# Pooling operands a block ahead, RWKV own products ahead of the chain

## The chip, the cores and the metric

The kernel runs on one core of one Trainium2 chip. Five engines work side by side: TensorE (PE), VectorE (DVE), ScalarE (ACT), GpSimd (POOL) and SyncE (SP), which issues the DMAs. The metric is the device time of one execution in microseconds, as a median of several runs.

## The reference, cut to what matters

One layer of a streaming encoder on x of 4096 tokens x 1024 features, float32. One projection x @ w_in feeds four mixers of 256 columns each (RWKV-7, pooling, mLSTM, retention); their outputs are gated, concatenated, projected again and normalised. Of the two mixers that the change touches:

```python
def pool_mix(u, w_grp, scale):       # u (B,S,256), windows 2, 4, 8, 16, one per group of 64 columns
    means = [(hi[..., sl] - lo) / min(t1, win) ...]          # trailing means, from a running sum
    d = concatenate(means) - u
    return einsum('bsgc,gcd->bsgd', d, w_grp) * scale

def step(state, inp):                # RWKV-7, one token, per head: state is 64 x 64
    sa = einsum('bhvk,bhk->bhv', state, -kk_t)
    state = state * w_t + sa * ab_t + v_t * k_t
    return state, einsum('bhvk,bhk->bhv', state, r_t)
```

The pooled result is multiplied by z * sigmoid(z) of a gate projection.

## The kernel before, in words

Tokens are cut into 16 blocks of 256 (`TB`). The stages follow one another: pooling (0 to 246.6 us), retention (to about 660), mLSTM (to about 1242), RWKV (to about 1957, with a tail of the embedding work to 2090), embedding and output. Every float32 product of the projections is taken with operands split in two parts, high and low (`hi`, `lo`): ScalarE casts the raw tile to `hi`, VectorE or POOL subtracts it to give `lo` (`fetch`), and three matmuls make one product (`dense`, lines 145 to 147). All DMAs are issued by SP in one order. The order of instructions on each engine is set by a scheduler that follows the program's order and priorities; `soon()` raises a priority, `keep` holds the program's order.

*Pooling.* `dense(b)` loads x of the block (`load_x`, four tiles), makes `zu` (48 matmuls) and twice `zpg` (24 each, with the gates of the mLSTM); `mix(b)` makes the trailing sums `s` on POOL, the differences `dp` on VectorE, `yp` on TensorE (8), multiplies by the gate `spg` on VectorE and by `pl_scale` on POOL, and stores y. Beside this, from block 2 on, one job a block of the list `todo`: the right operands of retention (`rB1`, `rB2`, `rB4` to `rB7`) are quarters of `w_rt` and differences of quarters. `sums` loads four quarter rows, forms four differences on POOL and stores them to DRAM (`T4` to `T7`); `right` reads quarters and differences back and splits them. `sums` also does this for `w_ml`, to be read by the mLSTM.

*RWKV.* Iteration i runs the string `ORDER` from left to right. Words name a stage with the lag of its block (`la`, `k`, `r`, `g`, `v` are dense groups through the `mm` PSUM banks, `n/2` takes two pieces); `vt` turns v and copies it to the tile `SAV`; `s`, `p` make `st`, `gp`; `inv`, `iv`, `pt`, `px`, `pu`, `py` invert a triangular matrix X in steps; `C` is one step of the chain of block i-2. A chain has four chunks of 64 tokens with three steps each: (1) `ry`: the state against `AR`, and the chunk's own products `g1` x `SAV` added (line 258 names all matmuls of RWKV), then the copy `R`; (2) `sa`, copied into `SAV`; (3) `ds`, the new state S, and the second half of `ry` to Y. `g1` of the own products are 64x64 blocks: the chunk's parity `e` chooses the array quadrant.

Of the kernel before, what the change touches and what calls it, by code (L numbers as in the profile page):

```python
# [42 lines left out]
class Trunk:  # L43
# [27 lines left out]
    def fetch(self, hi, lo, src, nm, eng):  # L71
# [4 lines left out]
        if self.spare % 2:  # L76
# [10 lines left out]
    def weights(self, name, g0, w=G, pool=None, bufs=5, gates=False):  # L87
# [30 lines left out]
    def load_x(self, b, more=None, between=None):  # L118

        his, los = [], []  # L120
        for k in range(0, KT, 2):
            p, n = (more, 3) if more is not None and (4 * b + k // 2) % 8 in (1, 4, 7) else (self.xp, XB)
# [69 lines left out]
    def _rwkv_out(self, es):  # L192
# [344 lines left out]
        def pt(b):  # L537
# [3 lines left out]
            V.transpose(out=Z.rearrange("p a c -> p (a c)"), in_=X.rearrange("p a c -> p (a c)"))  # L541
# [7 lines left out]
            A.copy(out=TD[:, :, 0:16], in_=t)  # L549
# [3 lines left out]
        def px(b):  # L553
# [14 lines left out]
        def pu(b):  # L568
# [3 lines left out]
            V.transpose(out=Z.rearrange("p a c -> p (a c)"), in_=X.rearrange("p a c -> p (a c)"))  # L572
# [5 lines left out]
            for e in range(2):  # L578
                A.copy(out=T[low(e)], in_=t[low(e)])
# [4 lines left out]
        def py(b):  # L584
# [5 lines left out]
            for e in range(2):  # L590
                V.tensor_copy(out=X[top(e), :, 32:64], in_=t[top(e)])
            yield 0.6
        def chain(b):

            eC, bon, AR, SAV, ST, g1, sg = (bl[b][n] for n in ("eC", "bon", "AR", "SAV", "ST", "g1", "sg"))
            Y = p2.tile([P, 2, G], F32, name=f"Y{b}", tag="Y")
            for c in range(4):
# [19 lines left out]
                with self.soon():  # L617
# [3 lines left out]
                    A.copy(out=SAV[cc][bs, e], in_=sa[bs].rearrange("p a v -> p (a v)"))  # L621
                yield True
# [92 lines left out]
    def pooling(self, es):  # L715
        nc, tc, a = self.nc, self.tc, self.a
        pool = lambda name, **kw: es.enter_context(tc.tile_pool(name=name, reuse_waits="tile", **kw))
        ws = pool("pws", bufs=1)
# [3 lines left out]
        p2 = pool("p2", bufs=2)  # L722
        self.mm = pool("pmm", bufs=4, space=PSUM)
# [12 lines left out]
        scale = self.load(cp, "pl_scale", a["pl_scale"].partition_broadcast(P))  # L736
        gbias = self.load(cp, "gbias", a["gbias"].partition_broadcast(P))
# [20 lines left out]
        def mix(b):  # L758
# [29 lines left out]
            V.scalar_tensor_tensor(out=Yp, in0=yp, scalar=0.5, in1=spg, op0=ALU.mult, op1=ALU.mult)  # L788
# [932 lines left out]
```

## Time and profile before

| | before |
|---|---|
| median of 3 runs | 2820.2 us (2818.15 to 2822.43) |
| the profiled execution | 2818.06 us, span 2816.3 us |
| TensorE busy | 2683.2 us, 95% |
| VectorE busy | 2166.8 us, 77% |
| ScalarE, POOL busy | 1104.5 us (39%), 1160.2 us (41%) |
| DMA moved | 281.14 MB |

A busy time counts the instructions of an engine in a stretch; matmuls are pipelined, so a start and the next start tell more than a duration. A row `A <- B` of a wait names the engine that stood idle and what released it. The time between the span and the execution, 1.8 us, lies outside the recorded program.

### The profile page before, as it was taken

Reading aid. Unit: us, or ns where it says so; the run is one execution under the profiler, and the core shown is the slowest. Engines: PE = TensorE matmul, PEld = TensorE weight load, DVE = VectorE, ACT = ScalarE, POOL = GpSimd, SP = SyncE. Lnnn points to the kernel's source line nnn. Section 1 sums busy time; section 2 is a strip of 40 time slices with the busy share of each in tenths; the row PEclk is TensorE's granted clock in tenths of the full one; section 3 lists DMA queues with packets and bytes.
Section 4 is the critical chain, followed back from the end, with each engine's and each line's share of the span. In section 5 each row is a group of like instructions: output and inputs, shape, how many; then the busy total and the mean of one; then the engine's idle time right before and its main releaser. Section 6 shows DMA issues by size and latency. Waiting matters only on the chain.

```text
span 2816.3 us, 57672 instructions
## 1 busy us (share of the span) xinstructions
PE 2683.2 (95%) x21940; PEld 2408.3 (86%) x21940; DVE 2166.8 (77%) x5239; ACT 1104.5 (39%) x2644; POOL 1160.2 (41%) x1295
## 2 busy tenths in 40 slices
PE   8899999998999999988999999999998999999997
PEld 7798888887899999978999999999887888778885
DVE  5666888887777787876888888888555566689997
ACT  2423222233666666653344434444222333422221
POOL 6555555553443344421232323333234111256665
PEclk9899999999999999989999999999999999999998
DMA  7753212213311111231111111113347444633431
GB/s 230 225 152 110 64 57 61 68 53 104 107 61 57 53 57 57 81 104 31 49 39 49 39 49 39 50 39 98 118 161 232 146 135 137 224 141 145 162 143 67
DMA packets 250501, 281.14 MB, mean 100 GB/s; under 512 B 69488, under 2 KB 166512, under 8 KB 250224
## 3 DMA queue, kind: packets, MB, share of 16 engines
q1 hardware_dynamic: 250224, 277.46, 31.4%
q8 instruction: 172, 2.82, 0.4%
q14 instruction: 105, 0.86, 0.1%
HBM read 209.69 MB, written 67.70 MB: 98 GB/s over the span
## 4 chain that ended last, share of the span: by engine, by line
PE 65%; DVE 15%; DMA 5%; POOL 4%; issue 4%; ACT 2%; SPq 0%; POOLq 0%; DVEq 0%; ACTq 0%
PE ry L258 3%; PE zqk L145 2%; PE zqk L147 2%; PE zqk L146 2%; DVE ro L1613 2%; DVE ro L1592 1%; PE sa L258 1%; PE zg L154 1%; DVE ro L1595 1%; PE zra L1406 1%; PE zg L156 1%; PE zg L155 1%; POOL ro L1596 1%; PE zrb L1407 1%; PE zrc L1406 1%
## 5 line engine op out<-in xcount | busy, mean ns | idle before, releaser
L1371 ACT CAST Ah<-xr 128x512 fp32r<-128x512 f32 x189 | 117.2, 621 | 278.6 <-PE zrb L1407 58.7
L1372 DVE TENSOR_TENSOR Al<-xr,Ah 128x512 fp32r<-128x512 f32 x135 | 99.0, 734 | 78.6 <-ACT Ah L1371 75.0
L651 POOL TENSOR_TENSOR SAV<-SAV,bon 64x256 f32<-64x256 f32 x64 | 42.7, 668 | 282.9 <-PE ry L258 272.4
L146 PE MATMUL zqk<-xl,wh_w_ml 128*128 128x256 f32 x512 | 148.7, 290 | 0.3 <-DVE xl L1062 0.3
L145 PE MATMUL zqk<-xh,wh_w_ml 128*128 128x256 f32 x512 | 148.2, 290 | 0.8 <-ACT xh L1061 0.8
L147 PE MATMUL zqk<-xh,wl_w_ml 128*128 128x256 f32 x512 | 147.7, 289 | 0.0
L85 DVE TENSOR_TENSOR xl<-rawx,xh 128x512 fp32r<-128x512 f32 x148 | 123.1, 835 | 31.6 <-ACT xh L84 30.7
L84 ACT CAST xh<-rawx 128x512 fp32r<-128x512 f32 x148 | 91.9, 621 | 139.6 <-DMA rawx<-in_xT 71.0
L1372 POOL TENSOR_TENSOR Al<-xr,Ah 128x512 fp32r<-128x512 f32 x54 | 70.9, 1313 | 132.8 <-ACT Ah L1371 72.0
L1596 POOL TENSOR_TENSOR ro<-ro,ln_b 128x512 f32<-128x512 f32 x64 | 100.7, 1594 | 53.8 <-DVE ro L1595 53.8
L849 POOL TENSOR_TENSOR rot<-rot,sw 128x256 f32<-128x256 f32 x64 | 69.4, 1084 | 93.9 <-DVE sw L848 89.1
L146 PEld LDWEIGHTS zqk<-xl,wh_w_ml 128*128 128x128 f32 x512 | 98.1, 192 | 2.3 <-DVE xl L1062 0.5
L145 PEld LDWEIGHTS zqk<-xh,wh_w_ml 128*128 128x128 f32 x512 | 97.9, 191 | 2.5 <-ACT xh L1061 1.0
L147 PEld LDWEIGHTS zqk<-xh,wl_w_ml 128*128 128x128 f32 x512 | 98.0, 191 | 1.1
L433 DVE SCALAR_TENSOR_TENSOR g<-gp,rc,c_rmask 128x128 f32<-128x128 f32 x256 | 70.9, 344 | 31.5 <-PE gp L258 31.5
L145 PE MATMUL zu<-xh,wh_w_pl 128*128 128x256 f32 x256 | 78.9, 308 | 15.7 <-ACT xh L84 10.0
L1391 POOL TENSOR_TENSOR xr<-xr,xr 128x512 f32<-128x512 f32 x27 | 35.2, 1302 | 141.2 <-DVE xr L1388 141.1
L146 PE MATMUL zu<-xl,wh_w_pl 128*128 128x256 f32 x256 | 78.1, 305 | 11.0 <-DVE xl L85 11.0
L1171 DVE SCALAR_TENSOR_TENSOR xc<-zc,c_convw,xc 128x256 f32<-128x256 f32 x192 | 87.6, 505 | 0.5
L634 DVE SCALAR_TENSOR_TENSOR S<-ds,eC,Se 64x64 f32<-64x64 f32 x256 | 72.4, 283 | 19.1 <-PE ds L258 14.4
L258 PE MATMUL ry<-SAV,g 64*64 64x64 f32 (+1 forms) x1024 | 83.5, 223 | 0.0
L659 POOL TENSOR_TENSOR Y<-Y,SAV 64x256 f32<-64x256 f32 x64 | 50.2, 784 | 75.7 <-DVE Y L655 65.8
(1127 smaller groups left out, 10578.9 us busy)
## 6 DMA issues: line engine op xcount, KB each, us to landing
rawx<-in_xT SPq DMA_DIRECT2D x148, 256.0 KB, 3.3
xr<-in_xT SPq DMA_DIRECT2D x108, 256.0 KB, 2.9
mr<-in_xT SPq DMA_DIRECT2D x64, 256.0 KB, 3.1
rp<-in_x SPq DMA_DIRECT2D x64, 256.0 KB, 3.2
s<-rp SPq DMA_DIRECT2D x64, 256.0 KB, 2.5
yo<-y SPq DMA_DIRECT2D x16, 1024.0 KB, 4.9
ro<-s SPq DMA_DIRECT2D x16, 1024.0 KB, 5.0
out<-ro SPq DMA_DIRECT2D x32, 512.0 KB, 2.6
```

The source lines that it names most:

```text
L84: nc.scalar.copy(out=hi, in_=raw)
L85: eng.tensor_tensor(out=lo, in0=raw, in1=hi.bitcast(F32), op=ALU.subtract)
L145: nc.tensor.matmul(out, lh(k), rh(k), start=(k == 0 and (apart or i == 0)), stop=False, skip_group_check=True)
L146: nc.tensor.matmul(out, lh(k), rl(k), start=False, stop=False, skip_group_check=True)
L147: nc.tensor.matmul(out, ll(k), rh(k), start=False, stop=(k == nk - 1), skip_group_check=True)
L258: mm = lambda *args, **kw: keep(nc.tensor.matmul(*args, **kw))
L433: V.scalar_tensor_tensor(out=g1[cc][:, hh, p, e], in0=gp[hh][:, p, e], scalar=rc[:, cc, e, i:i + 1], in1=msk[:, 64 * e:64 * e + P], op0=AL ...
L634: V.scalar_tensor_tensor(out=Sn[hv, p, hv], in0=ds[hv, p], scalar=eC[hv, p, c:c + 1], in1=Se[hv, p], op0=ALU.mult, op1=ALU.add)
L1171: V.scalar_tensor_tensor(out=xc[:, t], in0=zc[t // 2][:, t % 2, j:j + TB], scalar=cw[:, t, j:j + 1], in1=xc[:, t], op0=ALU.mult, op1=ALU.add)
L1371: self.nc.scalar.copy(out=hi, in_=src)
L1372: eng.tensor_tensor(out=lo, in0=src, in1=hi.bitcast(F32), op=ALU.subtract)
L1596: Q.tensor_tensor(out=rg, in0=rg, in1=ln["ln_b", g], op=ALU.add)
```

## The change

In pooling, x of block i+1 is loaded before `dense(i)`, and the tile pool `px` holds part of it. `todo`, with `sums` and `right`, is replaced by 16 units `half_row`, eight for `w_rt` and eight for `w_ml`, each of half a row's width: four loads one block ahead, the two direct operands split at the unit's block, four differences on POOL behind that block's sums, and the differences split (`w_rt`, without DRAM) or stored (`w_ml`) one iteration later. `plw` is multiplied by `pl_scale` and 0.5 once, so the per-block multiplication on POOL goes. The low parts of the gate weights are all made on VectorE, and the 8 mLSTM gate columns are loaded first.

In RWKV, the own products move out of the chain's step (1) into `own(b, cc)`, for two chunks at once, with the two quadrants alternating; it stands after `sa` of chunk 0 (for the block's second pair) and of chunk 2 (for the next block's first pair). `ry` now holds two chunks in one bank, twice; the dense banks `MM` go from 3 to 2. Iteration 1 runs another string, `FIRST`. The copies and transposes between `pt`, `px`, `pu` and `py` get `soon()`, and the last copy to X goes from VectorE to ScalarE.

```diff
-MM = 3
+MM = 2
+FIRST = "la.0 k.0 r.0/2 l.0 r.0/3 n.0 r.0 vt.1 m.0 g.0 bn.0 s0.0 p0.0 s1.0 p1.0 inv.0 v.0/2 pt.1 v.0/2 px.1 v.0/2 pu.1 v.0/1 py.1 v.0 iv.0"
...
-            for e in range(2):
-                V.tensor_copy(out=X[top(e), :, 32:64], in_=t[top(e)])
+            with self.soon():
+                for e in range(2):
+                    A.copy(out=X[top(e), :, 32:64], in_=t[top(e)])
             yield 0.6
+        def own(b, cc):
+            ry = ch.tile([P, 2, 2, P], F32, name=f"ry{b}_{cc}", tag="ry", bufs=2)
+            g1, SAV = bl[b]["g1"][cc], bl[b]["SAV"][cc]
+            for p in range(2):
+                for hh in range(2):
+                    for e in range(2):
+                        ks, bs = slice(64 * e, 64 * e + 64), slice(64 * (1 - e), 64 * (1 - e) + 64)
+                        hv = slice(64 * hh, 64 * hh + 64)
+                        mm(ry[bs, e, p, hv], g1[ks, hh, p, e, bs], SAV[ks, e, P * p + 64 * hh:P * p + 64 * hh + 64],
+                           start=(p == 0 and hh == 0), stop=False, skip_group_check=True)
...
-                    for p, hh, hv in heads:
-                        mm(ry[bs, p, hv], g1[cc][ks, hh, p, e, bs],
-                           SAV[cc][ks, e, P * p + 64 * hh:P * p + 64 * hh + 64], start=False, stop=False,
-                           skip_group_check=True)
...
+                if c == 0:
+                    own(b, 1)
+                if c == 2 and b + 1 < self.NB:
+                    own(b + 1, 0)
...
+        V.scalar_tensor_tensor(out=plw, in0=plw, scalar=0.5, in1=scale.rearrange("p (a v) -> p a v", a=2),
+                               op0=ALU.mult, op1=ALU.mult)
...
-            V.scalar_tensor_tensor(out=Yp, in0=yp, scalar=0.5, in1=spg, op0=ALU.mult, op1=ALU.mult)
-            Q.tensor_tensor(out=Yp, in0=Yp, in1=scale.unsqueeze(1).broadcast_to([P, 2, G]), op=ALU.mult)
+            V.tensor_tensor(out=Yp, in0=yp, in1=spg, op=ALU.mult)
...
+        def half_row(name, u):
...
+            for i, (kh, nh) in self.RIGHT.items():
+                t[i] = ws.tile([P, G], F32, name=f"w{i}{name}{u}", tag=f"w{i}", bufs=2)[:, :w]
...
+                keep(nc.sync.dma_start(out=t[i], in_=a[name][:, 4 * kh + k, o:o + w]))
+            yield
...
+            if name == "w_rt":
+                split(1, 1)
+                split(2, 2)
+            for i, o, x, y in diffs:
+                keep(Q.tensor_tensor(out=t[o], in0=t[x], in1=t[y], op=ALU.subtract))
+            yield
+            for i, o, x, y in diffs:
+                if name == "w_rt":
+                    split(i, o)
+                else:
+                    keep(nc.sync.dma_start(out=self.T[name][i][:, k, cs], in_=t[o]))
...
         for i in range(self.NB + 1):
+            if i + 1 < self.NB:
+                xs[i + 1] = self.load_x(i + 1, more=px if i + 2 < self.NB else None)
+            if i == 0:
+                next(units[0])
+            else:
+                next(units[i - 1], None)
+            if i + 1 < self.NB:
+                next(units[i + 1])
             if i < self.NB:
                 dense(i)
             if i >= 1:
                 mix(i - 1)
-            for _ in range(1 if i < self.NB else len(todo)):
-                if todo and i >= 2:
-                    todo.pop(0)()
+            if i < self.NB:
+                next(units[i])
```

The DMA queue of SP in pooling, before: `rawx4_6` is the last quarter of block 4's x, `rawx5_0` the first of block 5's; `T` are the stored differences, `raww_rt` the re-read operands.

```order
L83 DMA rawx4_6_845<-in_xT 128x512
L1326 DMA T6w_rt_636<-w3w_rt30_1155 128x512
L1345 DMA raww_rt10_1324<-in_w_rt 128x512
L1345 DMA raww_rt11_1328<-in_w_rt 128x512
L712 DMA y1_73<-Yp1_630 128x2x256
L1326 DMA T4w_rt_634<-w2w_rt30_1153 128x512
L1345 DMA raww_rt13_1336<-in_w_rt 128x512
L1345 DMA raww_rt50_1497<-T5w_rt_635 128x512
L1345 DMA raww_rt12_1332<-in_w_rt 128x512
L1345 DMA raww_rt51_1501<-T5w_rt_635 128x512
L83 DMA rawx5_0_998<-in_xT 128x512
```

The same queue now, from the last quarter of block 5's x to the first of block 7's; `w0w_rt5` to `w3w_rt5` are the half-width reads of unit 5.

```order
L85 DMA rawx5_6_946<-in_xT 128x512
L85 DMA rawx6_0_1106<-in_xT 128x512
L736 DMA y2_74<-Yp2_915 128x2x256
L85 DMA rawx6_2_1112<-in_xT 128x512
L85 DMA rawx6_4_1118<-in_xT 128x512
L835 DMA w1w_rt5_958<-in_w_rt 128x256
L835 DMA w2w_rt5_960<-in_w_rt 128x256
L835 DMA w3w_rt5_962<-in_w_rt 128x256
L835 DMA w0w_rt5_964<-in_w_rt 128x256
L85 DMA rawx6_6_1124<-in_xT 128x512
L85 DMA rawx7_0_1284<-in_xT 128x512
```

Between two blocks' loads of x there stood nine rows, stores and re-reads among them; now there are four half-width reads and a store of y per block.

TensorE in RWKV at the chain's step (1) of block 5's third chunk, before: `ry5_2` is that chunk's state product and own product, `vt6` block 6's turned v, `zg7` the gate group of block 7.

```order
L156 MATMUL z7r_19484<-xh7_6_19357,wl_w_rw_0_14450 128x256
L258 MATMUL ry5_2_19615<-S0_14715,AR5_1_18158 128x128 x2
L258 MATMUL ry5_2_19615<-SAV5_1_18883,g15_1_18176 64x64 x4
L453 MATMUL vt6_19626<-c_ident_192,v6_19224 128x128 x4
L258 MATMUL sa5_2_19661<-R5_2_19622,X5_18583 64x64 x4
L154 MATMUL zg7_19667<-wh_w_rw_896_14819,xh7_0_19339 128x256
```

The same place now; `ry5_1` holds block 5's second pair of chunks, `ry6_0` block 6's first.

```order
L158 MATMUL z7r_19563<-xh7_6_19432,wl_w_rw_0_14531 128x256
L260 MATMUL ry5_1_19477<-S0_14796,AR5_1_18236 128x128 x2
L455 MATMUL vt6_19700<-c_ident_195,v6_19304 128x128 x4
L260 MATMUL sa5_2_19735<-R5_2_19696,X5_18665 64x64 x4
L260 MATMUL ry6_0_19741<-SAV6_0_19698,g16_0_18993 64x64 x8
L156 MATMUL zg7_19750<-wh_w_rw_896_14900,xh7_0_19414 128x256
```

The four own products of the chunk are gone behind its state product, and eight of the next block stand behind `sa`, directly after `vt`.

TensorE in iteration 1, before: `zg1`, `z1v` are dense groups of block 1, `st1`, `gp1`, `bn1` its products, `pt0` the first step of block 0's inverse.

```order
L156 MATMUL z1v_15351<-xh1_0_15041,wl_w_rw_512_14468 128x256
L412 MATMUL st1_0_15364<-c_ident_192,BK1_15278 128x128 x4
L154 MATMUL z1v_15351<-xh1_2_15047,wh_w_rw_512_14469 128x256
L155 MATMUL z1v_15351<-xl1_2_15046,wh_w_rw_512_14469 128x256
L156 MATMUL z1v_15351<-xh1_2_15047,wl_w_rw_512_14468 128x256
L154 MATMUL z1v_15351<-xh1_2_15047,wh_w_rw_512_14469 128x256
L155 MATMUL z1v_15351<-xl1_2_15046,wh_w_rw_512_14469 128x256
L156 MATMUL z1v_15351<-xh1_2_15047,wl_w_rw_512_14468 128x256
L258 MATMUL pt0_15378<-Z0_0_15376,g10_0_14815 32x16 x16
L258 MATMUL pt0_15378<-Z0_0_15376,g10_1_14816 32x16 x16
L258 MATMUL gp1_0_0_15412<-AR1_0_15279,BK1_15278 128x128
L258 MATMUL gp1_0_1_15413<-AR1_0_15279,BK1_15278 128x128
```

The same place now, from the end of `zg1` to `pt0`; six more rows each of `gp1_0` and `gp1_1` and the first nine of `z1v` are left out.

```order
L158 MATMUL zg1_15380<-wh_w_rw_896_14900,xl1_6_15139 128x256
L260 MATMUL bn1_15432<-rkw_14789,rk1_15374 64x2 x8
L414 MATMUL st1_0_15443<-c_ident_195,BK1_15359 128x128 x4
L260 MATMUL gp1_0_0_15449<-AR1_0_15360,BK1_15359 128x128
L260 MATMUL gp1_0_1_15450<-AR1_0_15360,BK1_15359 128x128
...
L414 MATMUL st1_1_15467<-c_ident_195,BK1_15359 128x128 x4
L260 MATMUL gp1_1_0_15473<-AR1_1_15361,BK1_15359 128x128
L260 MATMUL gp1_1_1_15474<-AR1_1_15361,BK1_15359 128x128
...
L156 MATMUL z1v_15500<-xh1_0_15122,wh_w_rw_512_14550 128x256
L157 MATMUL z1v_15500<-xl1_0_15121,wh_w_rw_512_14550 128x256
L158 MATMUL z1v_15500<-xh1_0_15122,wl_w_rw_512_14549 128x256
L260 MATMUL pt0_15515<-Z0_0_15513,g10_0_14896 32x16 x16
```

`bn1`, both `st1` and both `gp1` moved ahead of `pt0`; of `z1v`, twelve rows stand ahead of it instead of eighteen.

## Rows read from the trace of the kernel before

**Rows 1.** Busy time of each engine by stretch; instructions in brackets.
```profile
core 0: us, PE busy (x) PEld busy (x) DVE busy (x) ACT busy (x) POOL busy (x), PEclk, DMA share, GB/s
...
40.00:170.00 130.00, 108.74 (x831) 105.84 (x831) 83.79 (x126) 42.83 (x81) 87.68 (x82) 0.92 0.73 222
170.00:246.60 76.60, 76.60 (x642) 76.59 (x642) 47.20 (x83) 24.91 (x47) 33.71 (x37) 1.00 0.37 114
0.00:246.60 246.60, 214.31 (x1657) 210.16 (x1658) 149.74 (x238) 82.46 (x152) 142.53 (x143) 0.94 0.62 190
...
1242.00:1957.00 715.00, 699.77 (x9283) 658.03 (x9284) 597.25 (x1843) 290.14 (x740) 212.81 (x357) 0.99 0.18 48
```

**Rows 2.** TensorE's waits in pooling: for what, us in total, times, longest.
```profile
PE zu L146 <- DVE xl L85: 11.0, 9, 4.1
PE zu L145 <- ACT xh L84: 10.0, 4, 6.1
...
PE zpg L145 <- ACT wh_w_pl L84: 3.8, 1, 3.8
```

**Rows 3.** The longest wait of all engines in pooling, same columns.
```profile
ACT xh L84 <- DMA rawx<-in_xT: 62.2, 16, 9.4
```

**Rows 4.** DMA issues in pooling by time: start, us, queue, line.
```profile
67.42 0.33 SPq L83 DMA_DIRECT2D rawx<-in_xT  x1
...
78.47 0.33 SPq L83 DMA_DIRECT2D rawx<-in_xT  x1
```

**Rows 5.** ScalarE in the same stretch, in order of time.
```profile
72.77 1.28 ACT L1346 CAST rB1whg<-raww_rt 128x512 fp32r<-128x512 f32 x2 [6.55 <-DMA raww_rt<-in_w_rt]
```

**Rows 6.** TensorE's first matmuls, in order of time.
```profile
5.66 0.58 PE L145 MATMUL zu<-xh,wh_w_pl 128*128 128x256 f32 x1 [5.66 <-ACT wh_w_pl L84]
...
12.08 0.28 PE L146 MATMUL zu<-xl,wh_w_pl 128*128 128x256 f32 x1
```

**Rows 7.** VectorE's two costliest forms, 40 to 170 us, then 170 to 246.6.
```profile
L85 DVE TENSOR_TENSOR xl<-rawx,xh 128x512 fp32r<-128x512 f32 x32 | 33.3, 1052 | 6.1 <-ACT xh L84 5.9
L781 DVE SCALAR_TENSOR_TENSOR dp<-s,c_pinv,us 64x256 f32<-64x256 f32 x34 | 25.5, 751 | 28.6 <-POOL s L767 22.8 <-POOL s L771 4.7 <-POOL s L768 0.6
...
L85 DVE TENSOR_TENSOR xl<-rawx,xh 128x512 fp32r<-128x512 f32 x23 | 22.0, 956 | 3.2 <-ACT xh L84 2.9
L781 DVE SCALAR_TENSOR_TENSOR dp<-s,c_pinv,us 64x256 f32<-64x256 f32 x25 | 14.2, 566 | 17.9 <-POOL s L767 16.9 <-POOL s L768 0.6
```

**Rows 8.** TensorE in RWKV around a `vt`, in order of time.
```profile
1516.56 0.67 PE L258 MATMUL ry<-SAV,g 64*64 64x64 f32 x8
1517.16 0.66 PE L453 MATMUL vt<-c_ident,v 128*128 128x128 f32 x4
1517.75 0.68 PE L258 MATMUL sa<-R,X 64*64 64x64 f32 x8
1518.35 0.39 PE L154 MATMUL zg<-wh_w_rw,xh 128*128 128x256 f32 x1
```

**Rows 9.** TensorE in RWKV, alternating small tiles, in order of time.
```profile
1538.01 0.69 PE L258 MATMUL pu<-Z,g 32*32 32x32 f32 x32 [0.15 <-DVE mvr L696]
1538.63 1.36 PE L258 MATMUL gp<-AR,BK 64*128 64x128 f32 x16
```

**Rows 10.** TensorE at block 1 of RWKV, in order of time.
```profile
1294.91 1.05 PE L258 MATMUL pt<-Z,g 32*32 32x16 f32 x64 [7.96 <-DVE Z L541]
1295.88 2.08 PE L258 MATMUL gp<-AR,BK 64*128 64x128 f32 x16
```

**Rows 11.** ScalarE after that `vt`, in order of time.
```profile
1517.91 1.51 ACT L457 COPY SAV<-vt 64x256 f32<-64x256 f32 x4 [0.27 <-PE vt L453]
```

**Rows 12.** All engines: last read of `z7v`, first matmul of `z8k`.
```profile
1589.17 0.48 DVE L1295 SCALAR_TENSOR_TENSOR v<-z7v,c_prm,v 128x255 f32<-128x255 f32 x1
...
1592.56 0.39 PE L154 MATMUL z8k<-xh,wh_w_rw 128*128 128x256 f32 x1
```

**Rows 13.** TensorE's waits in RWKV: for what, total, times, longest.
```profile
PE sa L258 <- DVE X L591: 1.4, 7, 0.2
```

More of the change, by code (lines that the diff above doesn't have):

```diff
@@ L121, in load_x @@
         for k in range(0, KT, 2):
-            p, n = (more, 3) if more is not None and (4 * b + k // 2) % 8 in (1, 4, 7) else (self.xp, XB)
+            p, n = (more, 2) if more is not None and (4 * b + k // 2) % 7 in (3, 6) else (self.xp, XB)
             lo = p.tile([P, 2, TB], F32R, name=f"xl{b}_{k}", tag="xl", bufs=n)
@@ L540, in pt @@
             Z = p1.tile([P, 8, 64], F32, name=f"Z{b}_0", tag="ZT")
-            V.transpose(out=Z.rearrange("p a c -> p (a c)"), in_=X.rearrange("p a c -> p (a c)"))
+            with self.soon():
+                V.transpose(out=Z.rearrange("p a c -> p (a c)"), in_=X.rearrange("p a c -> p (a c)"))
             t = ivp.tile([P, 8, 16], F32, name=f"pt{b}", tag="iv")
@@ L548, in pt @@
                            Z[q, i, 32 * u:32 * u + 16], start=True, stop=True)
-            A.copy(out=TD[:, :, 0:16], in_=t)
+            with self.soon():
+                A.copy(out=TD[:, :, 0:16], in_=t)
             yield 1.0
@@ L560, in px @@
                         mm(t[q, i], TD[q, i], X[q, i, 32 * u + 16:32 * u + 32], start=True, stop=True)
-            for e in range(2):
-                for u in range(2):
-                    q, c = rows(e, u), slice(32 * u + 16, 32 * u + 32)
-                    V.tensor_tensor(out=X[q, :, c], in0=X[q, :, c], in1=t[q], op=ALU.add)
+            with self.soon():
+                for e in range(2):
+                    for u in range(2):
+                        q, c = rows(e, u), slice(32 * u + 16, 32 * u + 32)
+                        V.tensor_tensor(out=X[q, :, c], in0=X[q, :, c], in1=t[q], op=ALU.add)
             yield 1.0
@@ L571, in pu @@
             Z = p1.tile([P, 8, 64], F32, name=f"Z{b}_1", tag="ZT")
-            V.transpose(out=Z.rearrange("p a c -> p (a c)"), in_=X.rearrange("p a c -> p (a c)"))
+            with self.soon():
+                V.transpose(out=Z.rearrange("p a c -> p (a c)"), in_=X.rearrange("p a c -> p (a c)"))
             t = ivp.tile([P, 8, 32], F32, name=f"pu{b}", tag="iv")
@@ L577, in pu @@
             T = p1.tile([P, 8, 32], F32, name=f"T{b}", tag="T")
-            for e in range(2):
-                A.copy(out=T[low(e)], in_=t[low(e)])
+            with self.soon():
+                for e in range(2):
+                    A.copy(out=T[low(e)], in_=t[low(e)])
             bl[b]["T"] = T
@@ L665, in _rwkv_out @@
             gens = {}
-            for w in ORDER.split():
+            for w in (FIRST if i == 1 else ORDER).split():
                 if w == "C":
@@ L717, in pooling @@
         pool = lambda name, **kw: es.enter_context(tc.tile_pool(name=name, reuse_waits="tile", **kw))
[L718 removed]
+        px = pool("px", bufs=2)
         wx = pool("wx", bufs=1)
@@ L722, in pooling @@
         p2 = pool("p2", bufs=2)
+        ws = pool("pws", bufs=1)
         self.mm = pool("pmm", bufs=4, space=PSUM)
@@ L787, in mix @@
             Yp = p2.tile([P, 2, G], F32, name=f"Yp{b}", tag="Yp")
-            V.scalar_tensor_tensor(out=Yp, in0=yp, scalar=0.5, in1=spg, op0=ALU.mult, op1=ALU.mult)
-            Q.tensor_tensor(out=Yp, in0=Yp, in1=scale.unsqueeze(1).broadcast_to([P, 2, G]), op=ALU.mult)
+            V.tensor_tensor(out=Yp, in0=yp, in1=spg, op=ALU.mult)
             self.store(b, 1, Yp)
-        self.rtB = {}
-        todo = [lambda k=k: self.sums(ws, "w_rt", k) for k in range(4)]
+        keep = tc.keep_in_program_order
@@ L794, in pooling @@
         qpair = lambda nm: [self.aq.tile([P, 4, H], F32R, name=f"{nm}{g}", tag="q") for g in range(2)]
-        todo += [lambda n=n: self.rtB.update({n: self.right("w_rt", n, (self.wpair if n in (1, 5, 2, 6) else qpair)(f"rB{n}"),
-                                                           lambda nm: ws.tile([P, H], F32, name=nm, tag=f"w{nm[-1]}"))})
-                 for n in (1, 5, 2, 6, 4, 7)]
-        todo += [lambda k=k: self.sums(ws, "w_ml", k) for k in range(4)]
-        for i in range(self.NB + 1):
+        self.rtB = B = {n: (self.wpair if n in (1, 5, 2, 6) else qpair)(f"rB{n}") for n in (1, 5, 2, 6, 4, 7)}
@@ new lines, in pooling @@
+        self.T["w_ml"] = {n: self.dr.tile([P, 4, 3 * P], F32, name=f"T{n}w_ml", tag=f"T{n}w_ml") for n in (4, 5, 6, 7)}
+        units = [half_row(name, u) for name in ("w_rt", "w_ml") for u in range(8)]
+        for i in range(self.NB + 1):
+            if i + 1 < self.NB:
[6 more added lines that the diff above has]
+                next(units[i + 1])
```

35 lines of the change are left out of this document (26 added, 9 removed).

## The prediction

> **What bounds the kernel now.** I read the busy times by stretch first, then what TensorE waits for in each stage, then the order of single instructions around those waits. TensorE is the engine of every stage: in RWKV it is busy 699.77 of 715.00 us and in the second part of pooling 76.60 of 76.60 [rows 1]. A saving therefore counts only where it takes TensorE's own time away or closes a hole in it. The reader should see two such places in [rows 1]. Pooling from 40 to 170 us is the one long stretch with holes: 108.74 busy of 130.00 at a clock of 0.92, DMA share 0.73, 222 GB/s; from 170 on the clock is 1.00 and there is no hole, at half the DMA share. RWKV has almost no holes, so only fewer or faster matmuls help there, apart from one hole that comes with block 1.
>
> The holes of pooling have one source. TensorE waits 11.0 us for `xl`, 10.0 for `xh` (the longest 6.1), and 3.8 for the gate weights [rows 2]. ScalarE, which makes `xh`, waits 62.2 us for the load of x, 16 times [rows 3]. On the DMA queue, which issues strictly in order, one load of x went out at 67.42 and the next at 78.47, with stores and re-reads of the differences between them [rows 4]. ScalarE has the same trouble: at 72.77 it starts a cast of a retention operand for whose load it waited 6.55 us, with casts of x behind it [rows 5].
>
> **Pooling.** The second stretch gives the full rate: 642 matmuls in 76.60 us, 0.119 each [rows 1]. A block is 48 of `zu`, 48 of `zpg` and 8 of `yp`, 104 in all, so 12.4 us; sixteen are 198.6. The trace shows 1657 of the 1664 in 246.60 us [rows 1], so pooling holds 48.0 us beyond that. What stays: 5.7 before the first matmul [rows 6], 3.8 for the gate weights [rows 2], whose loads are as many as before, and the slow first matmuls: 28 of them start between 5.66 and 12.08 [rows 6], 6.4 us where 28 x 0.119 is 3.3, so 3.1. That is 211.2; I allow 2 more for blocks 1 and 2, whose loads meet the weights. Pooling then ends at about 213 instead of 246.6: **33.5 us less**.
>
> Why the holes should close: in the new order the four loads of x stand a block earlier than their use, and between the loads of two blocks are four half-width reads (128 KB each) and a store of y. The 16 stores of differences of `w_rt` and the 24 reads of 256 KB in `right` are gone. A block then asks for 1.0 MB of x, 0.5 of weights, 0.25 of y, near 1.8 MB in 12.4 us, 145 GB/s (estimate from the tile sizes), where 222 were moved in the stretch with holes [rows 1]. The POOL multiplication by `pl_scale`, one per block, goes too; POOL is not the bound (87.68 of 130.00 [rows 1]), so its time is worth nothing by itself. Bounds: 36 if blocks 1 and 2 cost nothing, 16 if VectorE binds (below).
>
> The added VectorE work is the cover that might fail. Without operand splits VectorE needs 47.20 of 76.60 us [rows 1], 7.6 per 12.4 us block. Six half-width splits in each of the first eight blocks, each half of an `xl` of 956 ns [rows 7], add 2.9: 10.5. With the `xl` of 1052 and the `dp` of 751 ns of the first stretch, instead of 956 and 566 [rows 7], it is 7.6 + 4 x 0.10 + 4 x 0.19 + 6 x 0.53 = 11.9 of 12.4. That is under the block, narrowly; since x is loaded a block ahead, a late `dp` delays only `yp`. I take no loss and keep a rival for it.
>
> The same `xl` is slower where POOL is busier: 1052 ns at a POOL share of 0.67, 956 at 0.44 [rows 1, 7]. The Trainium skill, "GPSIMD Engine Reference" (section "1. Specifications"), says that GpSimd shares its SBUF interfaces with VectorE and that they contend when a VectorE instruction has two SBUF inputs; the rows agree in direction. By that page the removed multiplication speaks for the change and the POOL differences, now in the same blocks as the splits, against it; the sum is unchanged.
>
> **RWKV, own products.** Each of the 64 chain steps now issues `ry<-S,AR` and then the own products, 8 records of 64x64 in one quadrant of the array, from 1516.56 to 1517.16, 0.60 us [rows 8]. The change issues two chunks' worth together, 16 records, with the two diagonal quadrants alternating. The trace has no 64x64 of that form. Nearest is `pu`: 32 records of 32x32 alternating between two diagonal tiles, all in one PSUM bank as the own products are, 0.62 us to the next start, 19.4 ns per record or 0.61 ns per column [rows 9]; the own products now take 75 ns, 1.17 ns per column. `gp`, which alternates row halves, takes 1.36 for 16 records of 128 columns, 0.66 per column [rows 9]. At 0.61 the pair takes 16 x 64 x 0.61 = 0.62 instead of 1.20: 0.58 less, 32 pairs, **18.6 us**. Bounds: 18.6 and 0 (no overlap).
>
> Against that stands a wait. `own(b+1, 0)` is placed directly after `vt` and `sa`. `vt` ends and `sa` starts at 1517.75 and takes 0.60 [rows 8]; ScalarE copies the four pieces of `SAV` from 1517.91 in 1.51 us [rows 11], so the two that this own needs are there at about 1518.7, against the end of `sa` at 1518.35. I take 0.4 us for each of 15 blocks, 6 us; behind the waiting matmul stands the whole dense group `zg`. Net **13 us**, between 0 and 18.6.
>
> The Trainium skill, "TensorEngine Tiling (Array Packing)" (Restrictions and Gotchas, Gotcha 1), says that different row tiles cannot access the same PSUM bank at the same time. Here the two quadrants are different row tiles of one bank, so by it the own products would gain nothing. The trace speaks against the rule as a limit of speed, since `pu` has the same property and runs at half the time per column [rows 9]; the sum by the rule would be 13 us higher, and it is the first rival.
>
> **Two dense banks instead of three.** The new `ry` bank is paid by the dense pool. The tightest hand-over is from `v` to the next block's `k`: VectorE's last read of `z7v` starts at 1589.17 and takes 0.48, `z8k` starts at 1592.56 [rows 12]. That leaves 2.9 us, so nothing is lost in the steady state. In the last two iterations, where the plain blocks of the embedding use the same pool, it may cost up to 4 us; I take 0, since the chain's last steps stand earlier there.
>
> **Block 1's order.** TensorE waits 7.96 us at 1294.91 for block 0's first inverse transpose, and then runs 16 `gp` records at half clock in 2.08 us, against 1.36 elsewhere [rows 9, 10]. Now `bn`, both `st` and both `gp` stand ahead of that `pt`. From the rows near them (`gp` 1.4 to 2.1, of which there are two; `st` and `bn` I take at half a `gp` each, an estimate) they are 4 to 5 us, of which 0.7 is given back by six dense matmuls that move behind it. **4 us**, between 1 and 7.
>
> **The inverse's copies.** The last copy goes from VectorE to ScalarE (290.14 us busy of 715.00 against VectorE's 597.25 [rows 1]), and the steps before it get priority. The waits seen are small: `sa` for that X 1.4 us in 7 times [rows 13], `pu` 0.15 [rows 9], 13 such. **1.5 us**, between 0 and 3.
>
> **Sum.** 33.5 + 13 + 4 + 1.5 = 52. The profiled execution took 2818.1 us (a span of 2816.3 and 1.8 around it), so 2766.1 for its like; the median of the runs is 2.1 above it, so 2768.
>
> **Rivals.**
> (1) *The own products do not overlap*, or `zg` waits longer behind them: RWKV gains 0, and the total is 2768 + 13 = 2781. For: no 64x64 row of this form. Against: `pu`.
> (2) *VectorE becomes pooling's bound* in the first half. It already waits for POOL's sums, 16.9 us in 76.60 [rows 7], 2.7 a block; if it goes on losing these, 11.9 + 2.7 = 14.6, eight blocks lose 2.2 each: 18 us, total 2786. For: 96% load. Against: x is a block ahead.
> (3) *Slower than before: the third dense bank was needed.* If the evacuation of `v` came later than the hand-over allows, TensorE would stand in each of 15 blocks. It costs more than everything gained once the delay exceeds 2.9 + 52/15 = 6.4 us. At 7.0 it is 4.1 x 15 = 62, total 2830. For: VectorE has 83% load in RWKV, and its evacuations are queued in order. Against: the copies moved off it shorten just that queue.
> (4) *Pooling does not get shorter by what it should*, because the loads of block 1 and 2 collide with all weights (DMA 0.73 [rows 1]) or retention's first loads come late: gain 22 instead of 33.5, total 2780.
>
> **How the numbers follow.** Forecast 2768: 0.58. Rival 1: 0.12, rival 2: 0.13, rival 3: 0.04, rival 4: 0.10; 0.03 for a change whose parts cancel within 0.2% (about what a measurement of this kernel can tell from no change). The low end is all upper bounds together, 36 + 18.6 + 7 + 3 = 65: 2755. The high end takes in each of rivals 1, 2 and 4 alone and two of them together in part: 2794. Faster 0.93, same 0.03, slower 0.04.
>
> **What would show it.** Pooling: TensorE busy near 12.4 us per block from block 2 on, the first retention matmul near 213 us, no `xh` wait over 1 us. VectorE's share in 40 to 120 tells rival 2. RWKV: 16 own records from start to next start in 0.62 (right) or 1.20 (rival 1), a block shorter by 0.8 us, and a wait of `ry` for the `SAV` copy of some 0.4. Dense groups waiting for a read of their bank: rival 3. At the first `pt` a hole of 3 to 4 us. I am wrong if stages that the change leaves alone (mLSTM, output) move by more than 3 us.

## The result

The changed kernel takes 2777.3 us (median of 4 runs, 2776.6 to 2778.5) against 2821.3 us of the kernel before (4 runs of the same comparison, 2818.2 to 2822.5): a ratio of 0.9846, interval 0.9829 to 0.9863. Forecast was 2768, in 2755 to 2794. The gain is 44 us where 52 were forecast. The profiled execution took 2778.5 us, with a span of 2776.7 against 2816.3: 39.6 less.

To see where it comes from, I took the start of the same event in both traces and the difference of the two. A second profile of the changed kernel stands beside the first, since single stretches differ by some us from profile to profile.

| event (its time in before, us) | shift, changed kernel | shift, second profile | what happened since the row above |
|---|---|---|---|
| first retention matmul `zra` (246.7) | -30.2 | -29.8 | pooling: 30 gained, 33.5 forecast |
| first RWKV `z1k` (1263.8) | -26.1 | -27.6 | untouched stages: 4.1 and 2.2 lost |
| first `z2k` (1311.5) | -10.5 | -12.9 | iteration 1 (`FIRST`): 15.6 and 14.7 **lost**, 4 gained was forecast |
| first `z15k` (1920.3) | -28.5 | -29.3 | 13 blocks: 18.0 and 16.4 gained, 1.4 and 1.3 each |
| end of the span (2816.3) | -39.6 | -43.1 | tail: 11.1 and 13.8 gained, 0 forecast |

**Pooling.** The busy times by stretch of the changed kernel answer to [rows 1].

```profile
core 0: us, PE busy (x) PEld busy (x) DVE busy (x) ACT busy (x) POOL busy (x), PEclk, DMA share, GB/s
0.00:40.00 40.00, 31.78 (x233) 30.94 (x234) 25.43 (x48) 19.46 (x38) 15.64 (x23) 0.96 0.62 186
40.00:120.00 80.00, 79.64 (x666) 79.43 (x665) 59.30 (x118) 34.09 (x80) 45.64 (x54) 1.00 0.47 143
...
120.00:160.00 40.00, 36.59 (x291) 36.19 (x290) 25.19 (x46) 11.53 (x24) 28.22 (x35) 0.96 0.52 153
```

From 40 to 120 TensorE is full at clock 1.00, with 666 matmuls in 80 us (0.120 each), where before 831 in 130 (0.156) stood. The estimate of 145 GB/s is met by 143. What falls short lies between 120 and 160: its 291 matmuls are 34.7 us' worth at the full rate of 0.119, so 5.3 us are lost, 3.4 of them idle and most of the rest behind the second hole, where the granted clock is 0.50 from 146 to 149. The first 40 us hold 233 matmuls, 27.8 us' worth, and lose 12.2. TensorE's waits from 0 to 250 us, as [rows 2], name the causes:

```profile
PE zu L147 <- ACT wh_w_pl L86: 6.2, 1, 6.2
PE zu L148 <- DVE xl L87: 3.8, 3, 2.3
...
PE zpg L147 <- ACT wh_w_pl L86: 1.4, 1, 1.4
```

and the waits of all engines from 24 to 230 us (same columns) show which queue made `xl` late:

```profile
ACT xh L86 <- DMA rawx<-in_xT: 54.4, 22, 5.8
DVE dp L809 <- POOL s L795: 37.2, 12, 4.3
```

ScalarE still waits for x nearly as long as in [rows 3], but a block ahead, so TensorE has no `xh` wait left. VectorE stands 37.2 us in 12 waits for POOL's sums (39.7 in 12 in the same stretch of before), with the subtractions that make `xl` queued behind: rival 2's mechanism, at 3.8 us instead of 18.

**Iteration 1.** TensorE's first inverse transpose of block 0 (start, us; in brackets the idle time before and what ended it). It answers to [rows 10], where the wait was 7.96.

```profile
1285.69 1.05 PE L260 MATMUL pt<-Z,g 32*32 32x16 f32 x64 [13.29 <-DVE Z L544]
```

VectorE's instructions up to that `Z`, in order of time:

```profile
1277.32 0.16 DVE L503 TENSOR_TENSOR nt<-nt,xs 64x4 f32<-64x4 f32 x1 [3.54 <-DMA nt<-nd]
...
1283.87 0.58 DVE L503 TENSOR_TENSOR nt<-xs,nt 64x256 f32<-64x256 f32 x1
1284.48 0.41 DVE L528 TENSOR_REDUCE xs<-nt 64x32 f32<-64x256 f32 x1
1284.93 0.71 DVE L544 STREAM_TRANSPOSE Z<-X 128x512 f32<-128x512 f32 x1
```

The hole is 13.29 us. `Z` of block 0, which `pt` needs, comes on VectorE directly behind the whole series of `nt` and `xs`, and that series is the inverse of block *1*.

**The blocks.** TensorE around a `vt`, answering to [rows 8]:

```profile
1500.07 0.60 PE L455 MATMUL vt<-c_ident,v 128*128 128x128 f32 x4
1500.69 0.67 PE L260 MATMUL sa<-R,X 64*64 64x64 f32 x8
1501.18 1.07 PE L260 MATMUL ry<-SAV,g 64*64 64x64 f32 x16
1502.17 0.39 PE L156 MATMUL zg<-wh_w_rw,xh 128*128 128x256 f32 x1
```

From the start of `sa` to that of `zg` it is 1.48 us; before, `sa` with two chunks' own products took 0.60 + 2 x 0.60 = 1.80. TensorE waits for no dense bank anywhere between 1301 and 1892 us; its longest total there is 1.8 us in 8 times, for `S`.

### The profile page after: what moved, and what is told of

Read it like the earlier page. It is cut to its first block, busy times and chain, and to the rows that moved or that the text cites. A ratio compares the mean times of both kernels' runs of the same rounds, so it can differ in the third digit from the quotient of the medians.

```text
span 2776.7 us, 57736 instructions
## 1 busy us (share of the span) xinstructions
PE 2658.7 (96%) x21940; PEld 2388.0 (86%) x21940; DVE 2141.8 (77%) x5241; ACT 1111.4 (40%) x2700; POOL 1141.2 (41%) x1302
## 4 chain that ended last, share of the span: by engine, by line
PE 63%; DVE 18%; DMA 6%; issue 5%; POOL 5%; ACT 2%; SPq 1%; POOLq 0%; DVEq 0%; ACTq 0%
PE zqk L147 2%; PE zqk L148 2%; PE zqk L149 2%; PE ry L260 2%; DVE ro L1676 2%; DVE nt L503 2%; DVE ro L1655 1%; PE zg L156 1%; PE zpl L147 1%; DMA nd<-g 1%; PE zpl L149 1%; PE zpl L148 1%; DVE ro L1658 1%; PE zg L157 1%; PE zg L158 1%
## 5 line engine op out<-in xcount | busy, mean ns | idle before, releaser
L87 DVE TENSOR_TENSOR xl<-rawx,xh 128x512 fp32r<-128x512 f32 x148 | 116.4, 787 | 38.9 <-ACT xh L86 38.0
L156 PE MATMUL zg<-wh_w_rw,xh 128*128 128x256 f32 x256 | 77.4, 302 | 0.0
L655 POOL TENSOR_TENSOR Se<-S,eC 64x128 f32<-64x128 f32 x128 | 56.5, 441 | 48.7 <-DVE S L658 43.9
```

Source lines behind the costliest of these rows:

```text
L87: eng.tensor_tensor(out=lo, in0=raw, in1=hi.bitcast(F32), op=ALU.subtract)
L156: keep(nc.tensor.matmul(out, lh(k), rh(k), start=(k == 0 and i == 0), stop=False, skip_group_check=True))
```

## The experiments

Times are medians of 4 to 6 runs; ratios are against runs of the kernel before on the same chip (medians 2816.9, 2814.6 and 2814.0 in the three groups). Shifts are against the same event in the trace of before.

**1. The inverse of block 1 behind `py`**, else the changed kernel.

```diff
 FIRST = "... p1.0
-inv.0 v.0/2 pt.1 v.0/2 px.1 v.0/2 pu.1 v.0/1 py.1 v.0 iv.0"
+v.0/2 pt.1 v.0/2 px.1 v.0/2 pu.1 v.0/1 py.1 inv.0 v.0 iv.0"
```

> The changed kernel, but in FIRST the word inv.0 stands behind py.1, as in ORDER. Theory A: the hole of 13.3 us at the first pt comes from one shared buffer (nt of block 1's inverse and Z of block 0 use the same tile tag); with inv.0 ahead of pt.1 the transpose Z waits for the whole inverse of block 1 on VectorE. Then the hole shrinks below 2 us here and the total falls from 2777 to 2757 to 2762. Theory B: the hole comes from the bn, st and gp that FIRST puts ahead (their g products fill VectorE): then the hole stays above 8 us and the total stays within 5 us of 2777.

2771.1 us, 0.9832 (0.9815 to 0.9848). The hole is gone: this `pt` starts 13.8 us earlier and waits for nothing.

```profile
1271.92 1.05 PE L260 MATMUL pt<-Z,g 32*32 32x16 f32 x64
```

Iteration 1 loses 4.4 us (shift -28.0 to -23.6) instead of 15.6. The cause of the hole is the place of `inv.0`. Why the place matters is read from the program: `nt` of block 1 and `Z` of block 0 use one tile buffer (tag `ZT`, one copy), so the buffer goes to whichever is written first in the program. The trace above agrees, since VectorE idles 3.54 us for the DMA of `nt` with `Z` behind it, but no run here gives `Z` a buffer of its own. What is left is waits of the products that `FIRST` has pulled forward, from 1236 to 1289 us:

```profile
PE gp L260 <- DVE ST L415: 2.4, 2, 2.0
PE bn L260 <- POOL rk L386: 1.8, 1, 1.8
```

The total improves by 6 us only; in this profile the 13 blocks gain 13.6 instead of 16 to 18, with 3.2 us lost in block 7 at a granted clock of 0.93 (see the last section).

**2. The old order in iteration 1 too**, else the changed kernel.

```diff
-            for w in (FIRST if i == 1 else ORDER).split():
+            for w in ORDER.split():
```

> The changed kernel with ORDER in iteration 1 too (no FIRST). By the landmarks of the two traces iteration 1 lost 15.6 us. Both theories expect the loss to go: a hole of about 8 us as before the change, total about 2762. If FIRST as such were harmless and the 15.6 us came from own or from the two dense banks, it stays at 2775 or more.

2767.1 us, 0.9816 (0.9796 to 0.9836). `pt` waits 8.1 us, as before, yet iteration 1 loses only 1.7 (shift -27.9 to -26.2); experiment 3, which leaves RWKV as it was, loses 1.6 there too. `FIRST` therefore costs about 10 us between the medians and 13 to 14 in this stretch of the traces. Even mended it gains nothing: 4.4 lost against 1.7.

**3. Pooling alone**: before, with the changed pooling and nothing of RWKV changed.

> The kernel before with the pooling part alone. Theory: the part is worth what the first retention matmul shows, 30 us, and nothing of it is given back: 2791. Rival: the 4 to 5 us that the changed kernel lost between mLSTM's start and RWKV belong to this part (later loads, clock): 2795 to 2797.

2796.3 us, 0.9923 (0.9907 to 0.9939). `zra` is 29.8 earlier, `z1k` 29.6: the untouched stages lose 0.2 here. Two RWKV blocks of this profile, 3 and 5, lose 5.6 and 2.4 us (see the last section), and the last event stands at -23.3. The median meets the rival's number, but not for the rival's reason: what was lost was lost inside RWKV, not ahead of it.

**4. Own products alone**: before, with `own`, the new `ry` and two dense banks.

> The kernel before with own and the two dense banks alone (no FIRST, last copy to X still on VectorE). Theory: RWKV's blocks are shorter by 1.2 to 1.4 us each, and the tail keeps the gain of some 10 us that the changed kernel shows behind block 15: 2821 - 18 - 10 = 2793. Rival: the tail's gain comes from the copies and the pooling's other tile placement, so 2803; second rival: two dense banks cost in the tail, 2806 or more.

2790.8 us, 0.9905 (0.9889 to 0.992). The blocks gain 12.6 over 13 (shift -0.4 at `z2k`, -13.0 at `z15k`), 0.97 each. But the last `zoa` ends at -29.2: **16 us come from behind the blocks**, where own products cannot be more than two blocks' worth.

**5. The same pairs without alternation**: the changed kernel, with all eight records of one quadrant before those of the other.

```diff
-            for p in range(2):
-                for hh in range(2):
-                    for e in range(2):
+            for e in range(2):
+                for p in range(2):
+                    for hh in range(2):
```

> The changed kernel with own's loop over e outermost: the same 16 records in the same place, but eight in one quadrant and then eight in the other. Theory: the saving of own is the overlap of alternating quadrants, so 16 records take 1.1 to 1.2 us instead of 0.62 (where they wait for nothing), 26 pairs in 13 blocks give back about 11 us there, and the total is 2777 + 14 = 2791. Rival: the saving comes from issuing them beside sa (fewer changes of tile shape) and off the step before R; then the 16 stay near 0.7 and the total stays within 3 us of 2777.

2774.1 us, 0.9858 (0.9841 to 0.9874): as the changed kernel. My reason for the own products' gain, that two quadrants overlap, fell as the main cause. The pair behind `vt` in this kernel:

```profile
1496.85 0.68 PE L260 MATMUL sa<-R,X 64*64 64x64 f32 x8
1497.34 1.07 PE L260 MATMUL ry<-SAV,g 64*64 64x64 f32 x16
1498.33 0.38 PE L156 MATMUL zg<-wh_w_rw,xh 128*128 128x256 f32 x1
```

1.48 us again, to the hundredth. Here the pair is paced by something other than the order of quadrants, and ScalarE's copies of `SAV`, which end about there [rows 11], are the candidate. For the other pair of a block the next start comes 0.28 later than in the changed kernel (`sa` and own together 1.18 against 0.90). The block gain over 13 blocks is 15.7 (shift -14.5 to -30.2) against 18.0 and 16.4.

**6. Two dense banks alone** (`-MM = 3`, `+MM = 2`, else before).

> The kernel before with MM = 2 alone. Theory: nothing in the blocks of RWKV (0.0 us each, no wait for a dense bank); behind block 15 the order of the embedding's work changes, and the waits of 5.2 and 4.3 us for its first fast block's operands go or stay. If the changed kernel's gain behind block 15 comes from two banks, the total falls by 5 to 10 us to about 2809; if it comes from own, it stays at 2817 to 2821. Rival of the prediction (the third bank was needed): slower than 2825.

2807.6 us, 0.9973 (0.9962 to 0.9985). Nothing happens in the blocks (shift -2.0, -1.9, -1.9 at `z1k`, `z2k`, `z15k`): no third bank was needed, and rival 3 falls. But the last `zoa` ends at -10.4. The tail gains 8.5 us from a smaller pool.

**7. The inverse's copies alone** (`soon()` around them and the last one on ScalarE, else before).

> The kernel before with the priority of the inverse's copies and the last copy to X on ScalarE alone. Theory: the difference between the changed kernel's 1.3 us a block and own's 1.0 a block is this part: 0.3 us a block from the waits of sa for X and of pu, 4 to 5 us in all, 2814. Rival: it is worth the 1.5 us of the prediction or nothing: 2817 to 2820.

2805.0 us, 0.9963 (0.995 to 0.9976). The blocks gain 3.9 over 13 (shift +2.4 to -1.5), 0.3 each, and the tail gains 10.2 (-1.5 to -11.7). In before, TensorE's waits in these 13 blocks are the two that the prediction lists, `sa` for X (1.4 us in 7 times) and `pu`:

```profile
PE pu L258 <- DVE mvr L696: 2.0, 13, 0.2
```

In this run neither is left.

**What the tail is.** Three edits remove the same stall behind the last block: 6, 4 (which contains 6) and 7, which has nothing in common with them. Pooling alone (3) does not. TensorE's waits of before that are in question, from the first `z15k` to the last `zoa`:

```profile
PE zplb L1408 <- POOL Al L1372: 5.2, 1, 5.2
PE zpla L1406 <- ACT Ah L1371: 4.3, 1, 4.3
PE zpe L145 <- ACT wpwhg L84: 4.3, 1, 4.3
```

`Ah` is an operand of the embedding's gate:

```profile
2125.01 0.79 PE L1406 MATMUL zpla<-wg1whg,Ah 128*128 128x512 f32 x1 [4.29 <-ACT Ah L1371]
```

ScalarE casts `Ah` late because a cast of the gate weights, `gB`, stands ahead of it and waits 3.92 us for a sum on VectorE:

```profile
2118.76 0.62 ACT L84 CAST xh<-rawx 128x512 fp32r<-128x512 f32 x1
2123.30 0.62 ACT L1362 CAST gB<-w2w_gate 128x512 fp32r<-128x512 f32 x1 [3.92 <-DVE w2w_gate L1360]
2123.83 0.61 ACT L84 CAST xh<-rawx 128x512 fp32r<-128x512 f32 x1
2124.35 0.61 ACT L1371 CAST Ah<-xr 128x512 fp32r<-128x512 f32 x1
```

And VectorE is late because its operations take 1.75 us each there, where a few us earlier they took 0.68:

```profile
2113.90 0.68 DVE L1360 TENSOR_TENSOR w1w_gate<-w0w_gate,w1w_gate 128x512 f32<-128x512 f32 x1
...
2118.13 1.78 DVE L1449 SCALAR_TENSOR_TENSOR rp<-rp,ep 128x512 f32<-128x512 f32 x1
2119.83 1.77 DVE L85 TENSOR_TENSOR xl<-rawx,xh 128x512 fp32r<-128x512 f32 x1
2121.53 1.75 DVE L1360 TENSOR_TENSOR w2w_gate<-w2w_gate,w3w_gate 128x512 f32<-128x512 f32 x1
```

With two banks alone the casts of `gB` come earlier in ScalarE's order (its instructions in order of time), and `Ah` follows 9 us sooner without one ahead of it:

```profile
2106.55 0.62 ACT L1362 CAST gB<-w2w_gate 128x512 fp32r<-128x512 f32 x1 [1.08 <-DVE w2w_gate L1360]
...
2115.52 0.62 ACT L1371 CAST Ah<-xr 128x512 fp32r<-128x512 f32 x1 [0.82 <-PE zpl L146]
```

The waits of before for `Ah` (4.3), for `Al` (5.2) and most of that for `wpwhg` (4.3, now 0.5) are absent in the changed kernel. The order of the casts is set by the scheduler from what is ready when, so any edit that shifts the stages may move it. This gain is there once, whichever edit brings it. Between 2110 and 2170 us of before, where the waits for `Ah` and `Al` stand, the shift grows by about 13 us in experiment 4, 6 in 6 and 8 in 7, and by 10 in experiment 2, which has all these edits; in 3 it shrinks by 1.4, and the wait of 4.3 for `Ah` is still there. The medians agree in direction but do not show it by themselves: the gains of 3, 4 and 7, 0.0077 + 0.0095 + 0.0037 of the time, add up to 0.0209, or 59 us of 2815, and all of them together (2) give 0.0184, or 52, with 0.0013 to 0.0020 of uncertainty on each.

**8. The own products later**: experiment 2, with `own(b+1, 0)` behind step (3) of chunk 2 instead of behind `sa`.

```diff
-                if c == 2 and b + 1 < self.NB:
-                    own(b + 1, 0)
...
+                if c == 2 and b + 1 < self.NB:
+                    own(b + 1, 0)
```

> The changed kernel with ORDER in iteration 1 too, and own for the next block's first pair behind the third step of chunk 2 instead of directly behind its sa. Theory: the wait of own for the copies of SAV (0.3 us of each block by the trace: the 16 take 0.99 there) goes, 0.3 x 15 = 4 to 5 us below the kernel with ORDER alone (2767): 2763. Rival: the wait only moves to the next dense group or to ry, and nothing is gained: 2767.

2755.9 us, 0.9793 (0.9778 to 0.9807), the lowest median here; the interval of experiment 10 overlaps it. The 13 blocks gain 20.6 (shift -24.5 to -45.1), 1.58 each. The 16 own products now follow the state products `ds` and 8 records of `ry` of the same shape as `ds`:

```profile
1489.52 0.45 PE L260 MATMUL ds<-SAV,ST 128*64 128x64 f32 x8
1489.80 1.24 PE L260 MATMUL ry<-SAV,g 128*64 128x64 f32 x24
1490.97 0.39 PE L156 MATMUL zg<-wh_w_rw,xh 128*128 128x256 f32 x1
```

The last 16 of these records alone:

```profile
1490.36 0.68 PE L260 MATMUL ry<-SAV,g 64*64 64x64 f32 x16
```

From their start to that of `zg` it is 0.61 us: where nothing waits, the 16 take what the prediction gave as its sign of being right, 0.62. The median is 11 us below that of experiment 2, where 4 to 5 were forecast. The profiles bear out the forecast rather than the median: over the 13 blocks they differ by 5.2, of which 3.2 lie in block 7 of experiment 2. What else the median gained stays open.

**9. Experiment 8 without alternation** (the edit of 5 in it).

> As the run with ORDER alone and own late, but with own's loop over e outermost, so that its 16 records run eight in one quadrant and then eight in the other, here with no wait for the copies of SAV that could hide the difference. Theory: alternating quadrants is worth 0.28 us per 16 records where nothing waits (0.90 against 1.18 us for sa and own together), so 32 x 0.28 = 9 us: 2765 against 2756. Rival: quadrants of one PSUM bank do not overlap, and both orders take the same: 2756.

2768.0 us, 0.9843 (0.9825 to 0.9861). The 13 blocks gain 14.9 (shift -26.8 to -41.7), 5.7 less than in 8. The same instructions:

```profile
1488.97 0.45 PE L260 MATMUL ds<-SAV,ST 128*64 128x64 f32 x8
1489.25 1.52 PE L260 MATMUL ry<-SAV,g 128*64 128x64 f32 x24
1490.70 0.39 PE L156 MATMUL zg<-wh_w_rw,xh 128*128 128x256 f32 x1
```

and the last 16 alone:

```profile
1489.81 0.96 PE L260 MATMUL ry<-SAV,g 64*64 64x64 f32 x16
```

1.45 us to the next start against 1.17, and 0.89 against 0.61 for the 16 alone: alternating two quadrants is worth 0.28 us per pair where the pair waits for nothing, 26 pairs 7 us. The medians differ by more (12 us here, 10 against experiment 10, which ran in the same group); the traces explain 4 to 7 of it, and the rest stays open. The Trainium skill, "TensorEngine Tiling (Array Packing)" (Restrictions and Gotchas, Gotcha 1), has different row tiles unable to use one PSUM bank at the same time; by it 8 and 9 would be alike, and they are not.

**10. Loads of x first**: experiment 8, with `soon()` around the load of x of block i+1 in pooling.

> As the run with ORDER alone and own late, with the loads and splits of x in pooling raised in priority. The changed kernel still has two holes of 1.1 and 2.3 us at 129 and 147 us, where xl stands behind a dp that waits for POOL's sums on VectorE, and about 2 us of half clock behind them. Theory: it is the order of VectorE, so the holes go where xl moves ahead: 2 to 6 us less, 2750 to 2754, first retention matmul near 212. Rival: it is VectorE's and POOL's load, and something else waits as long: 2756, first retention matmul at 216.

2758.1 us, 0.9807 (0.9791 to 0.9822): no gain. `zra` stands at -31.7 against -30.5, TensorE's wait for `xl` is 3.6 us against 5.8 (3.8 in the changed kernel). The order of the loads isn't what is left in pooling. Whether the order on VectorE is remains untested: at the longest hole, 2.12 us at 144.5, the `xl` still stands behind a `dp` that waits 5.52 us for POOL's sums.

**11. The changed kernel again.**

> The changed kernel itself, on the chip of the two runs above, for their comparison and as a second profile of it: 0.985 of the kernel before, the hole of 13 us at the first pt again, and 1.3 us less than before in each block of RWKV; the places where mLSTM and the blocks lost 2 to 5 us in the first profile of it differ if they are chance.

2776.4 us, 0.987 (0.9855 to 0.9886). The loss in iteration 1, the gain per block and that of the tail repeat (table above). The loss between `zra` and `z1k` is 2.2 instead of 4.1. It falls mainly at the same two places in both profiles, between 690 and 760 us (1.4 here, 2.0 in the first) and behind 1170 (1.1 and 1.9); over the profiles of this study it lies between nothing and 5.6. So it is no effect of the change that I can show, and its cause stays open.

## Why the prediction came out as it did

**Pooling, 33.5 forecast, 30 measured: right in its mechanism and nearly in size.** The full rate holds where it was expected. The 3.5 us do not come from the start, for which 14.6 were allowed (5.7, 3.8, 3.1 and 2) and which lost 12.2. They come from the stretch from 120 to 160, where nothing was allowed and 5.3 were lost in the holes for `xl` and at half clock behind them. Rival 2 was a true mechanism with a price of 3.8 us plus some 2 at half clock; its condition, a late `dp` with `xl` behind it on VectorE, was priced as a load (11.9 of 12.4), when it is a matter of order in a queue. Rival 4 did not happen.

**Own products, 13 forecast, 0.97 per block measured, 14.5 for 15 blocks: right in size, for a reason that is only half right.** I derived 0.58 per pair from quadrants alone, and where nothing waits the 16 records do take 0.61 (experiment 8) instead of 1.20. But alternation gives only 0.28 of these 0.59, and only for a pair that doesn't wait. The other 0.31 comes from standing together: 16 in one quadrant take 0.89 (experiment 9), where two groups of 8 with products of another shape around each took 1.20. Behind `sa`, which has their shape, more is saved: without any alternation (experiment 5) one pair, with its `sa`, goes from 1.80 to 1.18 and the other to 1.48, 0.94 per block. In the trace the records of `sa` and of the first of these pairs even interleave at the border. The Trainium skill, "TensorEngine Tiling (Array Packing)" (Tiling Modes, Key Properties), says that a change of tiling mode drains TensorE; the 0.62 and 0.32 saved without alternation agree in direction. How much of it is the neighbours' shape and how much the place in the chain, no run separates. The step that failed is "Nearest is `pu`": `pu` is alternating and also 32 records in a row, and I gave the whole difference to one of the two. The wait for `SAV` was forecast at 0.4 and fits the 0.3 to 0.4 that the waiting pair lacks, but experiment 5 shows it hides the alternation as well.

**`FIRST`, 4 gained forecast, 15 lost measured: wrong in sign, and the largest error.** I counted the matmuls that were moved ahead of `pt` on TensorE, and took `Z` to come when it came before. The string also moved `inv.0` past `pt.1`. That is a move on VectorE and on a tile buffer: `nt` of block 1 and `Z` of block 0 share the tag `ZT`, so `Z` waited for 22 small operations and the DMA before them. What was pulled ahead also waits for operands of its own, 5.0 us in experiment 1 (`gp`, `bn` and `st`), so the 4 us were not there even without that hole. The step that failed is reading a move on one engine's order only. My test for it, "at the first `pt` a hole of 3 to 4 us", met 13.29.

**Copies, 1.5 forecast, 0.3 per block measured, 4.5 for 15 blocks.** The mechanism was right and the size too small: the two waits that I listed, 1.4 us for `sa` and 13 of 0.15 for `pu`, are 3.4 together, above my own upper bound of 3, and I took less than half of them. Experiment 7 has neither wait and gains 3.9 in the same blocks.

**Two banks: 0 in the blocks, as forecast.** The tail was forecast at 0 and gave 11 to 14 us. No row of the prediction covers it: I looked at the stages that the diff names, and missed that 13.8 us of waits stood in another (4.3, 5.2, 4.3), on an order that edits elsewhere changed.

**The sum.** Against 52 forecast, the profile has 30.2 - 4.1 - 15.6 + 18.0 + 11.1 = 39.6. Two errors of about 20 and 11 us, `FIRST` and the tail, have opposite signs; that the total came out near the forecast is partly luck. Rival 1's time, 2781, was nearly met for other reasons. The condition by which I would call myself wrong, 3 us in stages that the change leaves alone, was met in both profiles by the embedding's work behind the blocks, which gained about 8 and 10 us between 2110 and 2170. Between `zra` and `z1k` it was met once (4.1) and not in the second profile (2.2); there it was too tight for a stretch that varies by as much on its own.

## What to carry to other kernels

Where a change reorders steps, list for every step that is moved the engine *and the buffers* it takes: a shared single buffer hands itself out in program order, and a step that is pulled ahead can take it from one that is needed sooner. Put small matmuls of one shape together, and not directly behind the producer of their operand: a block gained 1.3 to 1.4 us with these products behind `sa` and 1.6 with them at the end of step (3). Try parts alone, and look at the end of the program too: a stall that depends on a scheduler's order can come or go with an edit elsewhere, and its gain is then credited to each edit that removes it.

## What the runs showed of the hardware

VectorE's operations of 128x512 took 0.68 to 0.69 us, and 1.75 to 1.78 in the stretch where GpSimd ran almost without a gap beside them: from 2116.0 to 2124.5 of the kernel before, VectorE is busy 8.50 of 8.50 us and POOL 8.34, and POOL's own take 1.60 to 1.75 against 1.29 at 2114.66. [rows 7] had shown 10%; here it is a factor of 2.6 for VectorE and 1.2 to 1.4 for POOL. The Trainium skill, "GPSIMD Engine Reference" (section "1. Specifications"), names the shared interfaces; it agrees, and the size is from these rows.

Single RWKV blocks lost more than their waits. In experiment 3 block 3 lost 5.6 us, where TensorE had waited 1.4 for `ST` and then ran 10 us at a granted clock of 0.50, the lower of its two levels (1.2 GHz). In experiments 1 and 2, whose blocks gain 1.3 otherwise, block 7 lost 3.2 and 1.8 behind the same wait, at a mean clock of 0.93 and 0.96. In block 5 of experiment 3, with the same wait and another of 1.2 for `X`, the clock stayed at 1.00 and only 2.4 were lost. What the four have in common is VectorE's order: the first step of the norm, `Y`, and an `xl` stand directly ahead of `ST`, as here in block 3 of experiment 3, while in the 165 others of blocks 2 to 14 in the thirteen profiles `ST` comes before that `Y`. So which block loses goes with the kernel's order and is no chance, though no run moves `ST` back to show it.

```profile
1369.72 0.68 DVE L708 TENSOR_TENSOR Y<-Y,mvr 128x512 f32<-128x512 f32 x1
1370.33 0.69 DVE L85 TENSOR_TENSOR xl<-rawx,xh 128x512 fp32r<-128x512 f32 x1
1371.05 0.69 DVE L413 TENSOR_TENSOR ST<-st,rc 128x512 f32<-128x512 f32 x1
1371.79 2.07 PE L258 MATMUL gp<-AR,BK 64*128 64x128 f32 x14 [1.42 <-DVE ST L413]
```

Why the clock fell behind three of these waits and not behind the fourth, no run shows.
